# The norm of x and the input product of its convolution as filler of the first recurrence

## The chip, the cores and the metric

One core of one Trainium2 chip runs the whole program. The metric is device time of one execution in microseconds (us), less is better. The engines named below are PE (TensorE: matmuls and, beside them, weight loads, PEld), DVE (VectorE), ACT (ScalarE), POOL (GpSimd) and SP (SyncE, which issues nearly all DMAs).

## What is computed

Two blocks in a row on a sequence of 256 tokens of width 1024. The change lies in the first layer of the first block. Each layer of that block has a context `ctx` and a sequence `x`. Both are normalised, modulated by adaLN vectors, and multiplied by `w_in`; the first 1024 columns of the product go to a gated convolution, the rest to a recurrence (RWKV) in two directions. The recurrence of `ctx` runs first, and its final states are the initial states of the recurrence of `x`.

```python
mod_x = (silu_c @ ada_w[l] + ada_b[l])[:, None, :]        # six vectors: sh1 sc1 gt1 sh2 sc2 gt2
mod_c = silu_cc @ ada_w[l] + ada_b[l]
ux = modulate(rmsnorm(x, norm1_g[l]), sh1, sc1) @ w_in[l]
uc = modulate(rmsnorm(ctx, norm1_g[l]), csh1, csc1) @ w_in[l]
prep_c = rwkv_prep(uc[..., CONV_IN:], *rw)
yc, s_f, s_b = rwkv_scans(prep_c, s_zero, s_zero, emit=not last)
prep_x = rwkv_prep(ux[..., CONV_IN:], *rw)
yx, _, _ = rwkv_scans(prep_x, s_f, s_b, emit=True)
mix_x = concatenate([conformer_conv(ux[..., :CONV_IN], *cv), rwkv_out(yx, prep_x, *post)])
x = x + gt1 * (mix_x @ w_out[l])
x = x + gt2 * swiglu(modulate(rmsnorm(x, norm2_g[l]), sh2, sc2), ffn_wg[l], ffn_wu[l], ffn_wd[l])
# and the same for ctx
```

## The kernel before

Activations lie feature-major: a tile is 128 features by 256 tokens, and a float32 matrix is carried as a high and a low part, so that a product of one 128 x 128 weight tile is three matmuls (`mm3`). Every weight block of 512 KB is loaded by a DMA on SP into one of four `raw` buffers and then split by ACT (line 341, `wh`) and DVE (line 342, `wl`). Only the adaLN weights go from `raw` to PE unsplit.

The kernel is written as one program in Python; a planner orders each engine's instructions when the program is built. It goes by program order as the priority and by the times at which its own model expects operands and buffers. On the chip every engine then follows that fixed order. So an instruction that stands late in the program can be put early where nothing ahead of it is expected to be ready, if its buffer is free. Tiles of one tag share a fixed number of buffers: `S` has 20 (`NS`, line 46), the PSUM tag `pb` two, `T1b` six, `Sb` two, `z` two, the convolution's `tap` two.

The first layer's recurrence over `ctx` is `wide(0, cf, None, QB, False, norm_x)` (line 1461). `rwkv` (mode "wide") makes the input product, per-pair operands `AR` and `BK`, a triangular inverse on DVE (`inverse`, a loop of 31 steps of two small operations at lines 961 and 963, then small matmuls into `Q`), the tiles `GR`, `KB` (`reads`) and `uv`, `r0` (`values`), and then four steps of `chain` for each of two groups. After each of these eight steps, `fill(FILL)` (line 919, `FILL` = 6) takes six steps from a generator of other work, the filler. In the program before, the filler is `conv_in` of `ctx` (line 659; four steps, each a product with two weight blocks, a sigmoid on ACT, a multiply on DVE) and then `ada_steps` (line 478; sixteen steps, for the adaLN vectors 2 to 5: eight halves of four weight blocks each, every half a PSUM tile, a copy to `T2b` on ACT at line 497, eight tiny matmuls into a second PSUM tile and an add on DVE at line 503). All PSUM tiles of the filler are of tag `pb`.

At "post" (line 924), once the chain's steps are in the program, `norm_x` loads x into two `z` tiles, normalises it (`rms_blocks`, line 409), transposes it on PE (line 438, four `pb` tiles of four transposes) and writes it as four `S` tiles (`feature_major`, line 428, by the list `EVAC1`: a scaling into `T1b` on ACT or DVE, a high part on ACT at line 460, a low part on DVE or POOL at line 462). Behind it stand the recurrence's own group norm and gate (which load `gup`, line 927, into another `S` tile), the convolution of `ctx` (`conv`, line 700: taps on POOL, DVE and ACT), `mixed_in`, then `conv_in` of x into `zx` (lines 1468 to 1470; its adaLN list is empty), `w_in` of x, `out` for `ctx` (`wout`, line 1475), and the recurrence of x.

The `S` tiles are asked for in this order: input product (3), `dup`, `iup`, two `sg`, four `BK`, `Lo`, four `AR`, `tj`, `X`, then four pairs of `GR` and `KB`, `qt`, `qc`, two `Q` (line 984), `yall` (line 902), the four of x's norm, and `gup`.

Of the kernel before, what the change touches and what calls it, by code (L numbers as in the profile page):

```python
# [37 lines left out]
NPOOL, NPOOLE, NPOOLC = (14, 3), (12, 4), (30, 0)  # L38
NTAP = 2

QB, QE, QC, EVERY = (2, 3, 4, 5), (2, 3, 4, 5), (1,), 2

FILL = 6
LATER = 1500
# [214 lines left out]
class Prog:  # L259
# [1151 lines left out]
    def first(self):  # L1411
        nc = self.nc
        self.setup()
        RW = list(range(NRW))
        KWV = [4, 5, 6, 7, 8, 9, 10, 11, 12]
        drain = lambda g: [None for _ in g]
        alone = {"r": ("ps", "acc00", "acc01"), "t": ("acc10", "acc11"), "b": ("pb",), "c": ("acc11",), "cs": ("acc10",)}
        beside = {"r": ("ps",), "t": ("ps",), "b": ("pb",), "c": ("pb",), "cs": ("pb",)}
        self.pstags = {"r": ("ps", "pb", "acc00", "acc01", "acc10", "acc11"), "b": ("pb",)}

        fl = lambda t: t.rearrange("p (a b) -> p a b", a=4)
        z = lambda: self.t(self.pool, [P, 4, T], "z", bufs=2)

        def wide(l, x, s0, ada, perm, before=None):

            def filler():

                steps = itertools.chain(self.conv_in(l, x, fl(self.x[0])), self.ada_steps(l, ada))

                def fill(n=1):  # L1430
                    lane = self.lane
                    self.on("b")
                    for _ in range(n):
                        next(steps, None)
                    self.on(lane)

                return fill

            self.pstags = alone
            for at in self.rwkv(l, self.w_in(l, x, RW), s0, True, "wide", filler()):  # L1440
                if at == "post" and before is not None:
                    before()
            self.on("c")
            drain(self.conv(l, fl(self.x[0]), fl(self.x[1]), (NPOOL, NPOOLE)[l]))
            self.pstags = beside
            self.on("b")
            return self.mixed_in(fl(self.x[1]), self.y, perm)

        self.ada(0, (1, 0))
        cf = self.load("ctx")  # L1450
        nc.sync.dma_start(self.const[:, NCONST1:], self.ap["const"][:, NCONST1:])
        cf = self.norm1(0, cf, 1, False, self.xf)
        early = []

        def norm_x():
            zt = lambda: self.t(self.pool, [P, D], "z", bufs=2)
            self.on("b")
            early.append(self.norm1(0, self.load("x", [zt(), zt()]), 0, False, self.Sr, keep=True))
            self.on("r")

        cm = wide(0, cf, None, QB, False, norm_x)
        states = self.states
        self.on("b")
        (xf,) = early
        zx = z()
        mods = self.ada_steps(0, [q for q in (2, 3, 4, 5) if q not in QB])
        for _ in self.conv_in(0, xf, zx):
            next(mods, None)
            next(mods, None)
        drain(mods)  # L1470
        win = self.w_in(0, xf, RW)
        ux = next(win)
        drain(win)
        self.load("ctx", self.x)
        f = self.out(0, self.x, 1, cm)
        self.on("r")
        drain(self.rwkv(0, iter((ux, 0)), states, True, "half"))
        y = self.y
        self.on("b")
        acc = z()  # L1480
        self.go = False
        self.bg = self.conv(0, zx, acc, NPOOLC, True)
        self.mods, self.every = self.ada_steps(1, QC), EVERY
        self.ffn_add(0, self.x, 1, f)
        drain(self.mods)
        self.gn()
        self.ada(1, [q for q in (1, 0) if q not in QC])
        self.on("b")
        cf = self.norm1(1, self.x, 1, False, self.Sr, acc=True)
        self.on("r")  # L1490
        drain(self.rwkv(1, self.w_in(1, cf, KWV, "b"), None, False, "all"))
        states = self.states
        self.on("b")
        xm = self.mixed_in(acc, y)
        self.load("x", self.x)
        f = self.out(0, self.x, 0, xm)
        self.ffn_add(0, self.x, 0, f)
        self.on("r")
        for b in range(2):
            nc.sync.dma_start(self.keep[b], self.x[b])  # L1500
        xf = self.norm1(1, self.x, 0, True, self.xf, acc=True)
        xm = wide(1, xf, states, QE, True)
        for b in range(2):
            nc.sync.dma_start(self.x[b], self.keep[b])
        f = self.out(1, self.x, 0, xm)
        self.ffn_add(1, self.x, 0, f)
        self.rms_blocks(self.x, keep=True)
# [130 lines left out]
```

## Time and profile before

| | us |
|---|---|
| median of 3 runs | 2772.72 |
| lowest and highest of the runs | 2772.6 and 2775.5 |
| the profiled execution | 2776.2 |
| its span, first to last instruction | 2774.1 |
| mean granted TensorE clock of the profiled execution | 0.961 |

The span is what the rows below measure from; 2.1 us of the profiled execution lie outside it. A clock of 1.00 is 2.4 GHz and 0.50 is 1.2 GHz, the two levels that PE is granted. The first recurrence with everything around it lies between 110 and 440 us of the span.

### The profile page before, as it was taken

To read this page: it belongs to the slowest core of one execution; us is meant where nothing else is said; L and a number is where in the kernel's file an instruction comes from. 1 tells how busy PE (TensorE), PEld (TensorE's weight loads), DVE (VectorE), ACT (ScalarE), POOL (GpSimd) and SP (SyncE) were. 2 spreads that over 40 slices of the span, in tenths; PEclk is the share of its full clock that TensorE was granted. 3 is DMA by queue.
4 is the path that set the end of the run, shared out by engine and by line. 5 is a ranking of instruction groups with operands and counts; after the bars stand their busy time and mean duration, and the time that the engine had idled before them with its cause. 6 is when DMAs were issued, how large, how long until landed. Compare 5 with 4: busy or idle time off the path is not lost.

```text
span 2774.1 us, 53770 instructions
## 1 busy us (share of the span) xinstructions
PE 2628.3 (95%) x22398; PEld 2288.3 (82%) x22398; DVE 1713.4 (62%) x2703; ACT 1327.6 (48%) x2015; POOL 667.0 (24%) x669
## 2 busy tenths in 40 slices
PE   7889988999889998899899899999999999999998
PEld 4866867888678897866799899889899898889897
DVE  3885778655577555984555655666655655755655
ACT  5533654434564346433544544654544544644543
POOL 0287999920130001384200000010000000100000
PEclk9989989999999999979899999999999999999999
DMA  7244424434323354234355555524555554525653
GB/s 251 102 153 167 153 86 167 139 129 145 137 77 115 130 181 148 100 138 153 124 188 183 198 184 188 188 86 157 183 186 186 183 186 172 170 85 183 205 185 119
DMA packets 118767, 430.70 MB, mean 155 GB/s; under 512 B 13174, under 2 KB 13686, under 8 KB 118524
## 3 DMA queue, kind: packets, MB, share of 16 engines
q1 hardware_dynamic: 118524, 427.28, 44.7%
q8 instruction: 175, 2.87, 0.4%
q14 instruction: 68, 0.56, 0.1%
HBM read 425.13 MB, written 2.10 MB: 154 GB/s over the span
## 4 chain that ended last, share of the span: by engine, by line
PE 76%; DVE 10%; POOL 5%; ACT 5%; issue 2%; DMA 2%; SPq 0%; ACTq 0%; POOLq 0%; DVEq 0%
PE pb L333 32%; PE acc L333 24%; PE ps L333 19%; POOL tap L731 3%; DVE wl L342 2%; POOL z L732 1%; DVE T1c L725 1%; DMA raw<-in_ada 1%; DVE S L963 1%; DVE T L961 1%; POOL x L732 1%; ACT wh L341 1%; PE acc L438 0%; DMA raw<-in_wr 0%; ACT L384 0%
## 5 line engine op out<-in xcount | busy, mean ns | idle before, releaser
L342 DVE TENSOR_TENSOR wl<-raw,wh 128x1024 fp32r<-128x1024 f32 (+1 forms) x654 | 814.5, 1249 | 621.6 <-ACT wh L341 390.9
L341 ACT CAST wh<-raw 128x1024 fp32r<-128x1024 f32 (+1 forms) x654 | 681.8, 1046 | 892.7 <-PE pb L333 349.8
L333 PE MATMUL pb<-xf,wh 128*128 128x256 f32 (+1 forms) x2560 | 488.1, 289 | 15.6 <-DVE T1b L588 5.2
L333 PE MATMUL pb<-S,wh 128*128 128x256 f32 x2560 | 490.9, 289 | 4.3 <-DVE S L462 1.8
L333 PEld LDWEIGHTS pb<-xf,wh 128*128 128x128 f32 (+1 forms) x2560 | 411.3, 195 | 29.7 <-DVE T1b L588 8.8
L333 PEld LDWEIGHTS pb<-S,wh 128*128 128x128 f32 x2560 | 407.7, 192 | 21.5 <-issue 11.7
L333 PE MATMUL ps<-S,wh 128*128 128x256 f32 x2048 | 390.6, 288 | 0.5 <-ACT S L460 0.4
L333 PE MATMUL pb<-xf,wl 128*128 128x256 f32 (+1 forms) x1280 | 372.8, 292 | 8.9 <-DVE wl L342 8.9
L365 POOL TENSOR_TENSOR wl<-raw,wh 128x1024 fp32r<-128x1024 f32 x22 | 52.1, 2379 | 1340.7 <-ACT wh L364 824.2
L333 PE MATMUL pb<-S,wl 128*128 128x256 f32 x1280 | 367.4, 287 | 2.1 <-DVE wl L342 2.1
L333 PEld LDWEIGHTS ps<-S,wh 128*128 128x128 f32 x2048 | 327.0, 192 | 9.4 <-issue 3.7
L333 PE MATMUL ps<-S,wl 128*128 128x256 f32 x1024 | 293.8, 287 | 0.6 <-DVE wl L342 0.6
L333 PEld LDWEIGHTS pb<-xf,wl 128*128 128x128 f32 (+1 forms) x1280 | 249.3, 195 | 16.9 <-DVE wl L342 11.7
L333 PEld LDWEIGHTS pb<-S,wl 128*128 128x128 f32 x1280 | 245.3, 192 | 7.0 <-issue 3.2
L333 PE MATMUL acc<-wh,T 128*128 128x512 f32 x704 | 206.3, 393 | 0.0
L333 PEld LDWEIGHTS ps<-S,wl 128*128 128x128 f32 x1024 | 196.7, 192 | 3.0 <-issue 1.5
L333 PE MATMUL acc<-wh,T1b 128*128 128x512 f32 x528 | 158.6, 399 | 3.5 <-ACT T1b L341 3.5
L731 POOL TENSOR_SCALAR tap<-z,cols 128x255 f32<-128x255 f32 (+14 forms) x120 | 154.4, 1295 | 0.0
L333 PEld LDWEIGHTS acc<-wh,T 128*128 128x128 f32 x704 | 127.0, 189 | 23.6
L731 POOL TENSOR_SCALAR tap<-x,cols 128x246 f32<-128x246 f32 (+6 forms) x104 | 112.9, 1093 | 46.1 <-DVE x L670 46.0
L333 PEld LDWEIGHTS acc<-wh,T1b 128*128 128x128 f32 x528 | 94.9, 190 | 22.3 <-ACT T1b L341 4.4
L333 PE MATMUL acc<-wl,T 128*128 128x512 f32 x352 | 113.3, 395 | 0.0
(445 smaller groups left out, 3956.7 us busy)
## 6 DMA issues: line engine op xcount, KB each, us to landing
raw<-in_fu SPq DMA_DIRECT2D x132, 512.0 KB, 3.2
raw<-in_ada SPq DMA_DIRECT2D x96, 512.0 KB, 4.2
raw<-in_pu SPq DMA_DIRECT2D x88, 512.0 KB, 4.3
raw<-in_qu SPq DMA_DIRECT2D x88, 512.0 KB, 4.2
raw<-in_fd SPq DMA_DIRECT2D x66, 512.0 KB, 3.2
raw<-in_wr SPq DMA_DIRECT2D x51, 512.0 KB, 3.9
raw<-in_pd SPq DMA_DIRECT2D x44, 512.0 KB, 4.3
raw<-in_qd SPq DMA_DIRECT2D x44, 512.0 KB, 4.3
```

Of the source, the lines that this page charges most:

```text
L333: return self.nc.tensor.matmul(out, lhsT, rhs, start=start, stop=stop, **kw)
L341: self.nc.scalar.copy(hi, src)
L342: self.nc.vector.tensor_sub(lo, src, hi.bitcast(F32))
L365: self.nc.gpsimd.tensor_sub(lo, r, hi.bitcast(F32))
L725: nc.vector.scalar_tensor_tensor(av[:, d], z[:, f, s], w(j), av[:, d], ALU.mult, ALU.add)
L731: nc.gpsimd.tensor_scalar(t[:, d], z[:, f, s], w(j), None, ALU.mult)
L732: nc.gpsimd.tensor_add(zc[f][:, d], zc[f][:, d], t[:, d])
L961: nc.vector.tensor_mul(tv, tj[:, k + 1 : 32, k : k + 1].broadcast_to([P, m, k + 1]), X[:, k : k + 1, 0 : k + 1].broadcast_to([P, m, k + 1]))
L963: nc.vector.tensor_sub(X[:, k + 1 : 32, 0 : k + 1], X[:, k + 1 : 32, 0 : k + 1], tv)
```

## The change

The filler's second part becomes a generator that is passed to `wide`. For the first layer it is `then_x`: x's load and norm are one step; then `zx` is taken and the sixteen steps of adaLN run with the four steps of x's `conv_in` among them, one after the second of every four. The call at "post" and the loop behind `wide` that made x's `conv_in` go away. The second layer's `wide` gets the same sixteen adaLN steps as before. The first layer's filler has 4 + 1 + 16 + 4 = 25 steps of the 48 that are asked for, where it had 20.

```diff
-QB, QE, QC, EVERY = (2, 3, 4, 5), (2, 3, 4, 5), (1,), 2
+QC, EVERY = (1,), 2
...
-        def wide(l, x, s0, ada, perm, before=None):
+        def wide(l, x, s0, steps, perm):
...
-                steps = itertools.chain(self.conv_in(l, x, fl(self.x[0])), self.ada_steps(l, ada))
+                all_ = itertools.chain(self.conv_in(l, x, fl(self.x[0])), steps)
...
-            for at in self.rwkv(l, self.w_in(l, x, RW), s0, True, "wide", filler()):
-                if at == "post" and before is not None:
-                    before()
+            drain(self.rwkv(l, self.w_in(l, x, RW), s0, True, "wide", filler()))
...
-        def norm_x():
+        def then_x():
+
             zt = lambda: self.t(self.pool, [P, D], "z", bufs=2)
-            self.on("b")
             early.append(self.norm1(0, self.load("x", [zt(), zt()]), 0, False, self.Sr, keep=True))
-            self.on("r")
-
-        cm = wide(0, cf, None, QB, False, norm_x)
+            yield
+            early.append(z())
+            mods, conv = self.ada_steps(0, (2, 3, 4, 5)), self.conv_in(0, *early)
+            for i, _ in enumerate(mods):
+                yield
+                if i % 4 == 1:
+                    next(conv, None)
+                    yield
+            yield from conv
+
+        steps = then_x()
+        cm = wide(0, cf, None, steps, False)
+        drain(steps)
         states = self.states
         self.on("b")
-        (xf,) = early
-        zx = z()
-        mods = self.ada_steps(0, [q for q in (2, 3, 4, 5) if q not in QB])
-        for _ in self.conv_in(0, xf, zx):
-            next(mods, None)
-            next(mods, None)
-        drain(mods)
+        xf, zx = early
         win = self.w_in(0, xf, RW)
...
-        xm = wide(1, xf, states, QE, True)
+        xm = wide(1, xf, states, self.ada_steps(1, (2, 3, 4, 5)), True)
```

## Rows read from the trace of the kernel before

**Rows 1.** The page: the span, and busy time of each engine

```profile
span 2774.1 us, 53770 instructions
PE 2628.3 (95%) x22398; PEld 2288.3 (82%) x22398; DVE 1713.4 (62%) x2703; ACT 1327.6 (48%) x2015; POOL 667.0 (24%) x669
```

**Rows 2.** Windows by stage: stretch and length, then the columns of the heading

```profile
core 0: us, PE busy (x) PEld busy (x) DVE busy (x) ACT busy (x) POOL busy (x), PEclk, DMA share, GB/s
112.00:165.00 53.00, 42.45 (x496) 37.53 (x494) 48.60 (x101) 22.63 (x40) 31.10 (x31) 0.93 0.34 114
165.00:188.00 23.00, 22.70 (x186) 12.17 (x188) 21.03 (x56) 5.91 (x11) 14.70 (x15) 0.80 0.65 225
188.00:210.00 22.00, 22.00 (x382) 17.23 (x379) 10.85 (x16) 10.29 (x15) 19.16 (x23) 0.66 0.27 98
210.00:270.00 60.00, 58.41 (x803) 39.84 (x802) 35.26 (x73) 20.75 (x42) 47.19 (x54) 0.92 0.50 175
270.00:312.00 42.00, 42.00 (x261) 33.09 (x260) 26.78 (x44) 27.40 (x40) 38.28 (x40) 1.00 0.30 103
312.00:354.00 42.00, 41.55 (x312) 38.41 (x310) 31.44 (x46) 23.54 (x37) 41.38 (x42) 1.00 0.57 192
386.00:412.00 26.00, 14.97 (x205) 12.69 (x205) 24.02 (x38) 16.26 (x36) 25.92 (x20) 0.78 0.13 43
```

**Rows 3.** Timeline of POOL: the two clears of the `Q` tiles, line 986

```profile
188.18 0.95 POOL L986 MEMSET S<- 128x1024 f32 x1 [1.27 <-PE acc L333]
...
190.53 0.95 POOL L986 MEMSET S<- 128x1024 f32 x1 [0.72 <-DVE S L968]
```

**Rows 4.** Timeline of SP: loads of x, of its convolution's weights, of `gup`

```profile
107.06 0.33 SPq L1523 DMA_DIRECT2D z<-in_x  x1
...
242.83 10.43 SPq L348 DMA_DIRECT2D raw<-in_wc  x6
253.31 0.43 SPq L927 DMA_DIRECT2D S<-in_gup  x1
```

**Rows 5.** Windows of the adaLN matmuls alone: PE busy, loads, ACT, POOL, clock

```profile
166.70:211.00 44.30, 13.58 (x48) 1.58 (x48) 0.00 (x0) 0.00 (x0) 0.73 0.44 152
211.00:252.00 41.00, 16.59 (x64) 2.43 (x64) 0.00 (x0) 0.00 (x0) 0.90 0.60 211
```

**Rows 6.** The same for tile `T2b` (adaLN's tiny matmuls): PE, loads, ACT

```profile
166.70:211.00 44.30, 2.88 (x19) 2.62 (x20) 1.76 (x3) 0.73 0.44 152
```

**Rows 7.** Timeline of PE: adaLN matmuls of four weight blocks, and of one

```profile
159.04 1.92 PE L333 MATMUL pb<-raw,csil 128*32 128x512 f32 x16
...
177.27 1.05 PE L333 MATMUL pb<-raw,csil 128*32 128x512 f32 x4
```

**Rows 8.** Groups by line on PE, 252 to 312: transposes of x

```profile
L438 PE MATMUL pb<-const,z 128*128 128x128 f32 x12 | 1.7, 282 | 0.0
```

**Rows 9.** Windows between changes of the clock; columns as in rows 2

```profile
171.70:185.40 13.70, 13.45 (x142) 7.83 (x144) 11.80 (x32) 4.24 (x8) 8.46 (x9) 1.00 0.82 277
188.80:195.60 6.80, 6.80 (x163) 5.36 (x164) 6.47 (x8) 6.18 (x8) 6.08 (x7) 1.00 0.55 213
195.60:219.50 23.90, 23.90 (x258) 16.37 (x258) 12.67 (x26) 5.58 (x11) 20.36 (x26) 0.50 0.07 24
```

**Rows 10.** Timeline of PE: last matmuls of a `w_in` word, first of `wout`

```profile
351.04 0.40 PE L333 MATMUL pb<-S,wh 128*128 128x256 f32 x2
351.28 0.28 PE L333 MATMUL pb<-S,wl 128*128 128x256 f32 x1
351.40 0.86 PE L333 MATMUL acc<-wh,xf 128*128 128x512 f32 x3
```

**Rows 11.** Timeline of DVE: the last operation of `mixed_in` for ctx

```profile
316.47 0.47 DVE L342 TENSOR_TENSOR xf<-x,xf 128x256 fp32r<-128x256 f32 x1
```

**Rows 12.** Waits of PE, 112 to 165, and of all engines, 385 to 440

```profile
PE pb L333 <- DVE wl L342: 3.6, 3, 1.9
...
PE ps L333 <- DVE S L849: 3.4, 2, 2.8
```

More of the change, by code (lines that the diff above doesn't have):

```diff
@@ L1433, in fill @@
                     for _ in range(n):
-                        next(steps, None)
+                        next(all_, None)
                     self.on(lane)
```

## The prediction

> **What bounds the kernel now.** I read the page first, then windows by stage over the stretch that the change touches, then the timelines of single lines in it. PE is busy for 95% of the span [rows 1], so a change pays here only where it takes idle time or slow time from PE. The stage windows say where there is any [rows 2]. From 112 to 165 DVE is the bound (48.60 of 53 us, the inverse and the convolution's taps) and PE idles 10.55 us. From 165 to 188 DVE is still full (21.03 of 23) and PE is covered. From 188 to 354 PE is busy nearly throughout: 22.00 of 22, 58.41 of 60, 42.00 of 42, 41.55 of 42. Then, from 386 to 412, it idles 11 us behind the residual of `ctx` and its norm. So x's `conv_in`, which the change moves, stands in a stretch where PE has no gaps, and goes into one (210 to 270) where PE has 1.6 us of gaps. PE's work from 165 to 354 is a queue that is never empty: what counts is whether the new order makes PE idle, or lets it do the same work faster.
>
> **Part 1: x's load and statistics.** x is loaded at 107.06 [rows 4], although `norm_x` stands behind the chain in the program: the planner already put it where DMA and ACT had room. Nothing to gain there, 0 us.
>
> **Part 2: x's transposes and their evacuation.** Before, these came behind adaLN, because adaLN was ahead of them for the two `pb` buffers. Now they come ahead of it. The transposes themselves: 12 cost 1.7 us [rows 8], so 16 cost 2.3 us, and they can go into PE's idle time before 165 [rows 2]: **-2.3 us**. The evacuation is the point of this case. It writes four `S` tiles, and `S` is full. The clears of the two `Q` tiles show it: a clear needs no operand, only a buffer, yet POOL sat idle before the first until a matmul on PE, and before the second until the transpose of `X` on DVE [rows 3]: both waited for another `S` tile to be let go. In the order of the requests `yall` and then x's four tiles come next, so none of them can be had before 190.53. By the program the next ones let go are `qt` behind the inverse's first small matmuls, `BK` of pair 2, then `Lo` and `qc` behind its last ones (about 209), then `BK` of pair 3. `gup`, next in the order behind x's four, agrees: its load has no operand to wait for and is ahead in the program of x's `conv_in`, yet six blocks of that were issued before it, and it went at 253.31 [rows 4], when the first group's chain let its `AR` go. So x's high and low parts cannot be complete before about 210 to 216. Until then six `T1b` hold scaled tiles, the last transposed tile cannot be scaled and keeps one of the two `pb` buffers, and the other goes to the first half of adaLN, and then to x's first product, which waits for x.
>
> **Part 3: adaLN.** What follows is that between 166.7 and 211 only the first half of adaLN is left as filler, whose matmuls came at 159.04 before [rows 7]. Before, this stretch held 13.58 us of adaLN matmuls (12 blocks) [rows 5] and 2.88 us of tiny ones [rows 6], 16.5 us in all, and these now come behind 211. Not all of it is lost. From 188 to 210 PE was full and the inverse's small matmuls shared it with one block's 1.05 us and a pair's 1.9 us [rows 7], so the chain can start about 3 us sooner; and the last of `values`, about 3 us, can fill the room. I take 16.5 - 3 - 3 = **+10.5 us**. The ends: 0, if x's tiles get buffers sooner than I read, and 16.5.
>
> On the other side, blocks that wait for PE are cheaper than blocks that PE waits for. Two blocks of one half use different columns of the array: the 16 matmuls of four blocks took 1.92 us where they came together, 0.12 us each, and the 4 of one block 1.05 us where it came alone, 0.26 each [rows 7]. In 166.7 to 252 the 112 took 30.17 us [rows 5], nearly all alone; together they would take 13.4, so the gain lies between 0 and 16.8 us. Behind the change blocks pile up while the banks are held, but after the first few the fixed order again takes them as the planner expects them. I take a quarter: **-4 us**.
>
> The Trainium skill's page Perfetto Trace Analysis, section Optimization Strategy, speaks for and against the change at once: it advises interleaving stretches with different bounds, and says that bubbles which repeat can mean that there is no memory for the next tile. Rows 3 agree with the second; by the first alone part 3 would cost nothing.
>
> **Part 4: x's input product.** Eight blocks of 24 matmuls at 0.12 us, the pace of the last word of `w_in` [rows 10]: 23.0 us. They leave 259 to 309 and enter 211 to about 295, and PE is full in both: 0. Now their splits stand in the queues of ACT and DVE between the chain's own operations, and a product that waits for a low part holds the chain's matmuls behind it. The nearest row is the same work on `ctx`: 3.6 us of PE's waits for `wl` while DVE was full [rows 12]. DVE is at 35.26 of 60 in the chain [rows 2], so I take **+1.5 us** between 0 and 3.6. The eight DMAs change places with adaLN's on SP; at 0.50 DMA share [rows 2] that costs nothing.
>
> **Part 5: who waits for a later chain.** With 23 us of product and the adaLN of part 3 ahead of the chain's last two steps in priority, the chain ends up to 23.0 + 10.5 - 4 - 2.3 = 27 us later than before. Behind it come the group norm and `mixed_in`, whose last operation began at 316.47 [rows 11], and `wout`, which did not wait for it: PE reached it at 351.40, straight from `w_in` [rows 10]. The cover is 34.5 us, so this costs 0, and 1 us for each us by which the chain's delay exceeds 34.5. `gup` comes later with the chain, but is first needed after it.
>
> **Part 6: POOL.** The taps for x begin when those for `ctx` let go of the two `tap` buffers, with or without `zx`; an earlier `zx` can save at most POOL's 3.7 idle us of 270 to 312 [rows 2]. POOL's delay shows on PE once, in the 3.4 us wait for line 849 [rows 12]. I take **-1 us** between -3.4 and 0. Fewer switches between sigmoid and silu on ACT are covered by PE: 0.
>
> **The sum.** -2.3 + 10.5 - 4 + 1.5 - 1 = +4.7 us. The profiled execution's span goes from 2774.1 to 2778.8 us and its time from 2776.2 to 2780.9. The median lies 3.5 us under that execution, so I forecast 2777.4 us, slightly slower, and just under 0.2% (5.5 us), about what a measurement of this kernel can tell from no change. With the parts' own ends the forecast's case spans 2768 to 2787.
>
> **The rivals.**
>
> *Slower: the inverse is left bare.* Between 171.7 and 195.6 PE ran at 2.4 GHz but for one short stretch, and from 195.6 to 219.5 at 1.2 GHz [rows 9], where adaLN had thinned out and the inverse's small matmuls ran. If, without adaLN, the clock is down from about 172 on, the two full-speed stretches, 20.5 us, do half the work. About 10 us of it was adaLN's, which is gone; so the rest just fits, nothing is pulled forward, and the inverse's matmuls of 188.8 to 195.6 take some 4 us more. Then +16.5 + 4 - 2.3 + 1.5 - 1 = +18.7, without the gain from pairs: 2791 us. It decides from the point where less than 11 us of the 16.5 come back. For it speaks that PE has little else there; against it, that the clock came back to full twice in it [rows 9].
>
> *Faster: blocks in pairs.* If blocks arrive in pairs for most of the remaining 28, three quarters of 16.8 are -12.6 in place of -4: -3.9. If the product also lifts the clock as soon as it starts, some 8 us of the 23.9 at 1.2 GHz [rows 9] become 4: -8. So about 2765 us. Against it: the fixed order was built for blocks that come one by one.
>
> *Faster: the product holds the clock.* If the buffers come earlier than I read, x's product runs inside 195.6 to 219.5, the 23.9 us at 1.2 GHz become 12, part 3 costs nothing, and the sum is -12 - 2.3 + 1.5 - 1 = -13.8: 2759 us. The skill's page TensorE: Matmul & The Clock Gate, section HAM oscillation, says so as a rule: idle gaps of PE drop the clock, steady work keeps it. The trace agrees only in part: PE is shown busy for 23.90 of these 23.9 us [rows 9].
>
> *No effect.* The planner had hoisted x's load already and could keep the rest nearly as it was, with x's tiles behind adaLN for want of buffers: 2773 us.
>
> **How the numbers follow.** Forecast 0.47, bare inverse 0.24, pairs 0.12, clock held 0.10, no effect 0.07. The forecast's case lies within 0.2% with 0.33 of its 0.47, above with 0.12, below with 0.02. Faster by over 0.2%: 0.12 + 0.10 + 0.02 = 0.24; within: 0.33 + 0.07 = 0.40; slower: 0.12 + 0.24 = 0.36. The range is 2759 to 2793: it reaches the slower rival and the faster ones, and leaves out the chance that parts of two rivals add up.
>
> **What would show it.** Right: x's transposes near 160; its high parts (line 460) no earlier than 200; hardly any adaLN on PE between 170 and 210 and idle time or a low clock there; the chain's end near 290; `wout` starting straight after `w_in`, near 356. Part 2 is wrong if line 460 runs before 195. Part 5 is wrong if PE idles before `wout` for `mixed_in`. The sum is wrong, with its steps right, if PE takes the remaining blocks in pairs, or if the windows of 165 to 220 show another clock than I took.

## The result and the profile after

The changed kernel is slower: a median of 2808.78 us (2804.9 to 2812.5) against 2772.7 us of the kernel before on the same chip, a ratio of 1.0124 (95% interval 1.0104 to 1.0143). The forecast was 2777.4 us and its range ended at 2793. The profiled execution of the changed kernel, at the upper end of its runs, has a span of 2810.5 us, 36.4 more than [rows 1].

Here is what came of the rows ahead of the prediction. First the span and the engines, from the page of the changed kernel:

```profile
span 2810.5 us, 53763 instructions
PE 2650.6 (94%) x22398; PEld 2314.4 (82%) x22398; DVE 1712.9 (61%) x2703; ACT 1319.9 (47%) x2010; POOL 657.6 (23%) x669
```

The instructions of PE are as many as before, and they are busy 22.3 us longer; the other 14 us are idle time. The stage windows of the changed kernel (stretch and length, then busy time and count of PE, weight loads, DVE, ACT and POOL, granted clock, DMA share, GB/s) answer to [rows 2]:

```profile
112.00:165.00 53.00, 41.91 (x483) 38.22 (x482) 48.77 (x102) 22.97 (x41) 31.37 (x31) 0.90 0.26 92
165.00:188.00 23.00, 19.18 (x186) 15.35 (x185) 22.97 (x56) 9.03 (x16) 18.07 (x17) 0.65 0.37 137
188.00:210.00 22.00, 19.35 (x298) 16.80 (x298) 15.72 (x26) 8.73 (x13) 21.20 (x25) 0.50 0.01 3
210.00:270.00 60.00, 58.39 (x784) 43.49 (x784) 26.27 (x53) 17.83 (x37) 54.10 (x65) 0.90 0.46 161
270.00:312.00 42.00, 42.00 (x319) 28.76 (x315) 19.06 (x35) 14.58 (x23) 30.80 (x33) 0.96 0.67 237
312.00:354.00 42.00, 39.11 (x273) 34.72 (x273) 32.30 (x51) 24.13 (x39) 41.14 (x43) 0.96 0.41 141
```

From 165 to 210 PE idles 6.5 us where it idled 0.3, and the DMA share of 188 to 210 fell from 0.27 to 0.01: no weights are fetched, as the `raw` buffers hold blocks that wait. Windows of the adaLN matmuls alone (PE busy, its loads, ACT, POOL, clock) against [rows 5], and the two sides of the place where the clock came back, against [rows 9]:

```profile
166.70:211.00 44.30, 1.92 (x16) 0.42 (x16) 0.00 (x0) 0.00 (x0) 0.58 0.20 73
211.00:252.00 41.00, 7.17 (x32) 1.12 (x32) 0.00 (x0) 0.00 (x0) 0.86 0.36 129
252.00:305.00 53.00, 15.43 (x80) 2.43 (x80) 0.00 (x0) 0.00 (x0) 0.97 0.65 226
```

```profile
174.60:222.40 47.80, 40.10 (x580) 34.81 (x576) 36.82 (x70) 17.10 (x31) 44.51 (x47) 0.50 0.11 42
222.40:270.10 47.70, 47.70 (x597) 33.49 (x596) 18.64 (x39) 13.45 (x27) 43.76 (x52) 1.00 0.58 203
```

Four blocks of adaLN ran under the inverse where 16 had run (those of 159.04 and the twelve behind [rows 5, 7]). On the other side all 128 matmuls now take 1.92 + 7.17 + 15.43 = 24.5 us, against 1.92 + 13.58 + 16.59 = 32.1 before: they come in fours of blocks more often. The longest half-speed stretch doubled, from 23.9 to 47.8 us. Line 460, x's high parts, in the changed kernel (count, durations in ns, first and last start):

```profile
L460 ACT CAST S<-T1b x8: 401/404/408, 221.3 to 224.5; 128x256 fp32r<-128x256 f32 x8
```

And the timeline of the changed kernel at x's first squaring on ACT, at the weight loads and `gup` in SP's queue, and at the last matmul of `w_in` and the first of `wout`, against [rows 4, 10]:

```profile
111.84 0.64 ACT L416 ACTIVATE sq<-z 128x512 f32<-128x512 f32 x1 [1.14 <-DMA z<-in_x]
...
169.99 0.80 SPq L348 DMA_DIRECT2D raw<-in_wc  x2
170.88 63.55 SPq L348 DMA_DIRECT2D raw<-in_ada  x8
...
264.34 0.42 SPq L927 DMA_DIRECT2D S<-in_gup  x1
...
365.81 0.28 PE L333 MATMUL pb<-S,wl 128*128 128x256 f32 x1
365.93 0.86 PE L333 MATMUL acc<-wh,xf 128*128 128x512 f32 x3
```

The issues of eight loads of adaLN stretch over 63.55 us of the queue, from 170.88 on. `wout` starts at 365.93 in place of 351.40. So **14.5 us** arise up to `wout`. The other 22 us arise behind it, where the program's text did not change:

| us of the profiled execution | before | after | |
|---|---|---|---|
| D: x's first squaring to `wout` of ctx | 239.6 | 254.1 | +14.5 |
| A: from there to x's squaring in the second layer (1066.2; 1085.5) | 714.8 | 719.6 | +4.8 |
| B: from there to x's `wout` in that layer (1320.3; 1353.6) | 254.1 | 268.1 | +14.0 |
| C: from there to the end | 1453.8 | 1456.9 | +3.1 |

### The profile page after: what moved, and what is told of

It is laid out like the page before. It is cut to its first block, busy times and chain, and to the rows that moved or that the text cites. A ratio compares the mean times of both kernels' runs of the same rounds, so it can differ in the third digit from the quotient of the medians.

```text
span 2810.5 us, 53763 instructions
## 1 busy us (share of the span) xinstructions
PE 2650.6 (94%) x22398; PEld 2314.4 (82%) x22398; DVE 1712.9 (61%) x2703; ACT 1319.9 (47%) x2010; POOL 657.6 (23%) x669
## 4 chain that ended last, share of the span: by engine, by line
PE 78%; DVE 12%; ACT 4%; POOL 2%; issue 2%; DMA 2%; ACTq 0%; DVEq 0%; POOLq 0%
PE pb L333 33%; PE acc L333 25%; PE ps L333 20%; DVE wl L342 2%; DVE T1c L725 2%; DVE S L963 1%; DVE T L961 1%; POOL tap L731 1%; ACT wh L341 1%; POOL x L732 1%; PE acc L438 0%; DMA raw<-in_ada 0%; ACT L384 0%; DVE acc L619 0%; DMA raw<-in_wr 0%
## 5 line engine op out<-in xcount | busy, mean ns | idle before, releaser
L333 PE MATMUL pb<-xf,wh 128*128 128x256 f32 (+1 forms) x2560 | 485.1, 287 | 12.4 <-ACT T1b L585 4.2
L333 PEld LDWEIGHTS pb<-S,wh 128*128 128x128 f32 x2560 | 411.0, 194 | 25.8 <-issue 14.2
L731 POOL TENSOR_SCALAR tap<-z,cols 128x255 f32<-128x255 f32 (+14 forms) x120 | 147.0, 1233 | 0.0
```

Source lines behind the costliest of these rows:

```text
L333: return self.nc.tensor.matmul(out, lhsT, rhs, start=start, stop=stop, **kw)
L731: nc.gpsimd.tensor_scalar(t[:, d], z[:, f, s], w(j), None, ALU.mult)
```

## The experiments

All kernels are measured in these four stretches (the time ahead of D differs by a few us from run to run). The ratio is to the kernel before on the same chip, with its 95% interval.

| run | D | A | B | C | ratio |
|---|---|---|---|---|---|
| before | 239.6 | 714.8 | 254.1 | 1453.8 | |
| swap_vectors | 241.0 | 709.6 | 257.5 | 1453.7 | 1.0001 (0.9991 to 1.0010) |
| after | 254.1 | 719.6 | 268.1 | 1456.9 | 1.0124 (1.0104 to 1.0143) |
| after_swap | 255.1 | 716.5 | 260.6 | 1454.5 | 1.0102 (1.0084 to 1.0119) |
| after_fill8 | 255.1 | 716.5 | 262.1 | 1452.8 | 1.0091 (1.0076 to 1.0106) |
| after_fill5 | 254.0 | 717.8 | 260.7 | 1457.6 | 1.0090 (1.0075 to 1.0105) |
| norm_only | 241.2 | 719.6 | 259.6 | 1451.9 | 1.0028 (1.0014 to 1.0042) |
| norm_then_ada | 242.2 | 715.8 | 257.9 | 1453.9 | 1.0048 (1.0032 to 1.0065) |
| turns_late | 248.0 | 713.4 | 253.7 | 1454.2 | 1.0001 (0.9989 to 1.0013) |
| ada8_first | 248.2 | 710.1 | 269.0 | 1453.2 | 1.0062 (1.0043 to 1.0081) |
| own_after | 254.3 | 712.9 | 262.2 | 1458.9 | 1.0078 (1.0060 to 1.0097) |
| own_before | 250.0 | 717.8 | 259.1 | 1452.7 | 1.0054 (1.0033 to 1.0075) |
| product_no_dve | 243.1 | 710.4 | 264.9 | 1453.9 | 1.0014 (1.0000 to 1.0027) |
| conv_late | 224.1 | 736.4 | 260.7 | 1454.4 | 1.0011 (0.9995 to 1.0027) |
| fill5 | 238.3 | 715.0 | 265.1 | 1453.7 | 1.0045 (1.0030 to 1.0059) |
| fill8 | 242.9 | 721.9 | 270.2 | 1448.9 | 1.0082 (1.0067 to 1.0097) |

D is steady where the first part's order is kept: the changed kernel and its three variants lie between 254.0 and 255.1. Edits that move nothing of the change (swap_vectors, fill5, fill8) put it between 238.3 and 242.9, so a difference of 3 us in D says little. Three questions were put.

**Which of the three moves costs the 14.5 us?** First the norm alone, on the kernel before:

```diff
-steps = itertools.chain(self.conv_in(l, x, fl(self.x[0])), self.ada_steps(l, ada))
+steps = itertools.chain(self.conv_in(l, x, fl(self.x[0])), before, self.ada_steps(l, ada))
...
-cm = wide(0, cf, None, QB, False, norm_x)
+cm = wide(0, cf, None, QB, False, norm_x())
```

> The kernel before, with the norm of x as the filler's first step of the second part and nothing else moved: adaLN follows in a row, x's input product stays behind the recurrence. Theory (first place holds the banks, and the product in turn takes the second one): one bank is held by x's last transposed tile, but adaLN has the other to itself, so blocks go on one after the other; half of the cost up to wout, 5 to 9 us, wout at 356 to 361 us. Rival (the norm alone does it): wout at 364 to 368 us with a half-speed stretch of 45 us or more. Rival (the turns alone do it): wout at 349 to 354 us.

D came to 241.2, +1.6: the norm in front is nearly free, and the rival that lays it on the turns is right (`wout` at 349.8). Windows of this run, first of the clock, then of adaLN alone:

```profile
168.00:188.50 20.50, 19.65 (x135) 10.57 (x133) 14.59 (x41) 2.63 (x5) 13.33 (x14) 0.50 0.51 183
...
195.30:219.20 23.90, 23.43 (x339) 19.10 (x333) 15.40 (x29) 8.76 (x15) 20.42 (x24) 0.50 0.01 2
```

```profile
166.70:211.00 44.30, 10.41 (x32) 1.11 (x32) 0.00 (x0) 0.00 (x0) 0.59 0.38 137
```

From 160 to 225 us the mean clock is 0.65 in this run, 0.74 before and 0.58 in the changed kernel. So more than half of what the changed kernel lost in clock is here too, and yet D lost 1.6 us: adaLN went on, at the slow clock. The clock alone is not the price. Then the changed kernel without the turns:

```diff
-            for i, _ in enumerate(mods):
-                yield
-                if i % 4 == 1:
-                    next(conv, None)
-                    yield
+            yield from mods
             yield from conv
```

> The changed kernel without the turns: the filler takes the norm of x, then all sixteen adaLN steps in a row, then the four of x's input product. Theory (the product in turn waits for S): the product asks for a bank only when x is long there, adaLN goes through by the other bank as in the run with the norm alone, distance 239 to 245 us. Rival (the product in the chain): it is enough that the product stands ahead of the chain's last steps: 250 us or more.

D is 242.2, as the theory had it. The copies that end adaLN's halves (line 497) show the difference; up to 200 us the run without turns has three, the changed kernel one:

```profile
L497 ACT COPY T2b<-pb x3: 586/586/587, 171.4 to 189.4; 128x512 f32<-128x512 f32 x3
```

```profile
L497 ACT COPY T2b<-pb x1: 585/585/585, 170.9 to 170.9; 128x512 f32<-128x512 f32 x1
```

Then the turns, put off until behind five halves (turns_late), and the norm put off until behind four (ada8_first):

```diff
-                if i % 4 == 1:
+                if i > 8 and i % 2 == 1:
```

> The changed kernel with the turns put off: the filler takes the norm of x, then five halves of adaLN (ten steps), and only then x's input product in turns, one step behind each further half. Theory (PE's order under the inverse): the first product stands in PE's fixed order ahead of adaLN's second half and waits for operands from DVE, which the inverse keeps full until 188 us; put behind five halves it waits for nothing. Distance from x's first squaring to wout's first matmul 240 to 246 us (before 239.6, after 254.1, adaLN in a row 242.2), and three halves of adaLN copied out before 200 us. Rival (the turns themselves cost, by the banks or by the product ahead of the chain): 250 us or more.

```diff
+            mods = self.ada_steps(0, (2, 3, 4, 5))
+            for _ in range(8):
+                next(mods)
+                yield
             zt = lambda: self.t(self.pool, [P, D], "z", bufs=2)
...
```

> The changed kernel, but the filler takes eight adaLN steps (four halves) first, then the norm of x, then the other eight in turns with x's input product. Theory (first place holds the banks): the cost up to wout comes only from x's transposed tiles holding a pb bank while the S tiles are full, so that adaLN is missing under the inverse. With four halves ahead they run at 160 to 200 us as before, the half-speed stretch of PE between 160 and 225 is about 24 us long and not 48, line 460 comes at 200 to 225, and wout's first matmul at 349 to 354 us (before 351.4, after 365.9). Rival (turns): the alternation of adaLN blocks with the product is what costs, wherever the norm stands: wout at 360 or later. For the rest of the program, from wout's first matmul to the end (before 2422.7, after 2444.6 us): theory (order) says it moves by 5 us or more in either direction although its work is the same, rival (lateness) says it goes back to 2423 within 4 us, together a time of 2773 within 5 us.

248.0 and 248.2: between theory and rival in both, so both were incomplete. In turns_late the three halves came before 200 us as expected (the third at 195.9), and D still lost 5.8 us to the run without turns. Windows of the whole of D, in the kernel before, in the changed kernel, in turns_late and in norm_then_ada (columns as in the stage windows):

```profile
111.81:351.40 239.59, 226.70 (x2411) 176.64 (x2411) 171.91 (x328) 108.68 (x181) 189.21 (x201) 0.91 0.44 152
```

```profile
111.84:365.93 254.09, 232.02 (x2411) 187.79 (x2410) 171.55 (x328) 103.91 (x178) 208.38 (x222) 0.87 0.40 143
```

```profile
112.97:361.01 248.04, 231.74 (x2415) 187.28 (x2414) 170.53 (x328) 102.81 (x177) 196.72 (x211) 0.87 0.43 146
```

```profile
111.44:353.63 242.19, 225.95 (x2418) 180.58 (x2417) 168.51 (x328) 101.27 (x176) 198.50 (x211) 0.92 0.44 151
```

PE idles 12.9, 22.1, 16.3 and 16.2 us in them. Of the 14.5 us, 9.2 are idle time of PE, and for 5.3 its matmuls are busy longer, at a mean clock of 0.87 in place of 0.91. The step from turns_late to the changed kernel, 6.0 us, is idle time of PE (5.8 us): the price of a product ahead of adaLN's second half under the inverse. The step from norm_then_ada to turns_late, 5.8 us, is none: PE idles alike and is busy 5.8 us longer, at a mean clock of 0.87 in place of 0.92. So it is not made of waits for products among the steps of the chain, and products run there in norm_then_ada too (256.6 to 284.4, the chain's last state at 292.3). Why PE had the lower clock in this one execution stays open. What is left, 1.6 to 2.6 us for the norm, is no more than D moves by without it. The fourth half of ada8_first came out at 198.8 and the fifth at 236.1 (the norm now stands in the way behind 200 us), so its +8.6 is no clean repeat of either step.

**What does the product wait for?** The prediction said: for x's `S` tiles. A first pair gives x's norm a place of its own, in both kernels (and the scratch tile `sq` becomes bfloat16):

```diff
+            one = new([P, T], F32R)
+            hs = ls = [one.unsqueeze(1).broadcast_to([P, 4, T])] * 2
...
-early.append(self.norm1(0, self.load("x", [zt(), zt()]), 0, False, self.Sr, keep=True))
+early.append(self.norm1(0, self.load("x", [zt(), zt()]), 0, False, self.own, keep=True))
```

> The changed kernel, with x's norm written to memory of its own and not to S tiles. There is room for 1 KB per partition only, so all eight high and low parts go to one place over each other: the instructions and their sizes stay, the numbers that x's products read don't. Measured as the distance from x's first squaring to wout's first matmul (before 239.6, after 254.1, adaLN first 248.2, norm alone 241.2 us). Theory (the product in turn waits for S): with tiles of its own line 460 is done by about 175, x's product and adaLN both run under the inverse, the half-speed stretches between 160 and 225 add up to less than 30 us (after: 54.6), and the distance is 236 to 243 us. Rival (the turns themselves): the product's matmuls ahead of the chain cost, whatever it waits for: 250 us or more.

> The kernel before with the same memory of its own for x's norm, beside the run of the changed kernel with it. In the kernel before adaLN stands ahead of x's norm, so that nothing in the first recurrence waits for x's S tiles: distance from x's first squaring to wout's first matmul 237 to 242 us by both theories. The rest of the program, of which S tiles are freed earlier, is open by both, some 2420 to 2445 us.

The tiles did come earlier, and D did not move: 254.3. The mean clock of 160 to 225 us was 0.63 (0.58 in the changed kernel), which makes 48 of these 65 us at half speed where under 30 were expected. Here are the high parts in own_after (line 464 there) and the low parts on DVE (466), and then the timeline of PE at the product:

```profile
L464 ACT CAST xn<-T1b x8: 398/405/420, 158.8 to 184.5; 128x256 fp32r<-128x256 f32 x8
L466 DVE TENSOR_TENSOR xn<-T1b,xn x6: 407/410/473, 164.3 to 186.2; 128x256 fp32r<-128x256 f32 x6
```

```profile
186.74 0.79 PE L333 MATMUL pb<-xn,wh 128*128 128x256 f32 x2
...
192.06 0.40 PE L333 MATMUL pb<-xn,wh 128*128 128x256 f32 x2
194.24 0.73 PE L333 MATMUL ps<-S,S 32*32 32x32 f32 x18 [1.79 <-DVE S L973]
...
219.84 0.58 PE L333 MATMUL pb<-xn,wl 128*128 128x256 f32 x1
...
226.72 1.07 PE L333 MATMUL pb<-raw,csil 128*32 128x512 f32 x8
```

The last high part came at 184.5 and not at 224.5, so the full `S` was indeed what had held line 460. But behind it stood the next wait: four scalings and six low parts had to find room on DVE, which the inverse keeps full. The product began at 186.74, its second half at 219.84 behind the inverse's and `values`' matmuls in PE's fixed order, and adaLN's second half behind it at 226.72. The pair is not clean, as own_before missed its expectation by 8 us (250.0): with high and low parts in one place each must wait for the one before, 10.6 us in a row there. So a second run takes DVE out of x's product altogether:

```diff
+            if new == self.own and op == "l":
+                continue
+            e = "A" if new == self.own else e
...
+        if whole:
+            st = (self.raw(f"wc{l}", i) for i in range(8))
...
+                        self.mm(pu[:, j, :], w[:, k * P : k * P + P], x[k][0].bitcast(F32), k == 0, k == NF - 1)
```

> The changed kernel with an input product of x that needs nothing of DVE: x's tiles in the 1 KB of their own, scaled and written by ACT alone, without the low parts, and the product as one plain float32 matmul by the unsplit block in place of three by its parts (adaLN's blocks are multiplied so). The low parts of x are left out and its tiles lie over each other. Theory (the product waits for DVE): its first step runs before 182 us, adaLN's second half follows before 195, the half-speed stretches between 160 and 225 add up to 35 us or less (after 54.6), and the distance is 238 to 248 us, though the plain product itself is longer. Rival (the turns themselves): 252 us or more.

D is 243.1, with the same turns in the same places. PE in this run, at x's first product and the adaLN behind it, then the clock:

```profile
172.58 4.00 PE L333 MATMUL pb<-xn,raw 128*128 128x256 f32 x10
...
176.83 2.43 PE L333 MATMUL pb<-xn,raw 128*128 128x256 f32 x10
...
180.08 2.86 PE L333 MATMUL pb<-xn,raw 128*128 128x256 f32 x12
182.87 1.06 PE L333 MATMUL pb<-raw,csil 128*32 128x512 f32 x8
```

```profile
176.70:186.90 10.20, 9.85 (x118) 7.32 (x117) 10.16 (x21) 2.50 (x5) 6.72 (x7) 1.00 0.37 122
186.90:221.10 34.20, 33.91 (x458) 27.16 (x462) 20.02 (x40) 12.53 (x20) 30.13 (x36) 0.50 0.20 73
```

The product ran under the inverse and adaLN followed, though only half of the half (the rest at 209.99, not before 195), and the half-speed stretches were 41 us and not 35. Its window of D:

```profile
110.62:353.67 243.05, 231.95 (x2354) 182.13 (x2353) 155.68 (x310) 94.90 (x172) 193.96 (x215) 0.89 0.44 151
```

D fell by 11.0 us against the changed kernel, and PE's idle time in it from 22.1 to 11.1. So some 11 of the 14.5 us go with what the product needs of its operands, x's tiles and the split weights. The run doesn't only take a wait away: DVE does 18 operations less (155.7 us in place of 171.6) and ACT 9.0 us less, so wait and work are not told apart. The 3.5 us that stay with the turns are of the size by which D moves without them. The waits were under the inverse and not in the chain: from 220 to 366 us PE in the changed kernel waited once, and that for the shift behind `w_in`:

```profile
PE pb L333 <- DVE S L630: 2.9, 1, 2.9
```

How much is DVE's and how much is that of `S` in the changed kernel itself is not separated further: own_after took only `S` away, product_no_dve both.

**Where do the 22 us behind `wout` come from?** Two edits that change no work, only how many filler steps stand behind a step of the chain (in both layers' `wide`), on the kernel before:

```diff
-FILL = 6
+FILL = 5
```

> The kernel before with five filler steps behind a step of the chain in place of six: the same work, nearly the same order in the first recurrence, but the planner orders the rest of the program anew. Theory (order): wout's first matmul within 5 us of 351.4, and the rest from there on differs from 2422.7 us by 5 us or more, in either direction, with no cause in the edit. Rival (lateness): the rest is within 4 us of 2422.7 and the time within 5 us of 2773.

> The kernel before with eight filler steps behind a step of the chain in place of six: again the same work and a new order later on. Theory (order): wout's first matmul within 6 us of 351.4, and the rest differs from 2422.7 us by 5 us or more. Rival (lateness): the rest is within 4 us of 2422.7 and the time within 6 us of 2773.

A + B + C, 2422.7 before, became 2433.8 and 2441.0, and the ratios are 1.0045 and 1.0082: a re-ordering that does little to the first recurrence (D 238.3 and 242.9) costs up to 0.8%. In fill5 `wout` came at 345.2, 1.2 us further off than expected, as all ahead of D was 4.9 us shorter. The counterpart is an edit that leaves the order of the rest alone:

```diff
-QB, QE, QC, EVERY = (2, 3, 4, 5), (2, 3, 4, 5), (1,), 2
+QB, QE, QC, EVERY = (2, 3, 5, 4), (2, 3, 4, 5), (1,), 2
```

> The kernel before with two adaLN vectors of the first recurrence's filler in the other order (2, 3, 5, 4 for 2, 3, 4, 5): the same work, and an order of the engines that is the same but for those blocks, 120 lines of PE's, against 2600 to 5400 in the runs so far. Theory (order): the rest of the program keeps the order of the kernel before, so it keeps its time: distance to wout within 3 us of 239.6, rest from wout on within 3 us of 2422.7. Rival (any edit in this stretch, or the chip, costs the rest): 2428 us or more, as in the eight other runs (2427.6 to 2444.6).

2420.8, and a ratio of 1.0001. The same edits on the changed kernel:

> The changed kernel with eight filler steps behind a step of the chain in place of six: the same work, hardly another order in the first recurrence, the rest ordered anew. Theory (order): distance from x's first squaring to wout's first matmul within 4 us of 254.1, and the rest from wout on differs from the 2444.6 us of the changed kernel by 4 us or more, while it stays above the 2422.7 us of the kernel before as in the four runs so far (2431.1 to 2441.0). Rival (lateness): the rest stays within 3 us of 2444.6.

> The changed kernel with two adaLN vectors of the filler in the other order (2, 3, 5, 4 for 2, 3, 4, 5): the same work, and an order that differs from that of the changed kernel by 243 lines of PE's, all in the first part of the program. Theory (order): what the changed kernel lost behind wout belongs to the order that the planner made of the rest, so it stays here: distance from x's first squaring to wout within 3 us of 254.1, rest from wout on within 4 us of 2444.6, and a time of 2803 to 2813. Rival (the chip, or a single execution): the rest falls back by 8 us or more towards the mean of the other runs, 2431.

> The changed kernel with five filler steps behind a step of the chain in place of six: the same work, 2270 lines of PE's order other than in the changed kernel. Theory (order): distance from x's first squaring to wout within 5 us of 254.1, rest from wout on anywhere between 2421 and 2445 us, as in the runs so far, and 4 us or more from 2444.6. Rival (the rest is the late chain's own price): rest within 4 us of 2444.6.

The two FILL runs gave 2431.4 and 2436.1, away from 2444.6 as the order theory wants. But after_swap, which keeps the order of the changed kernel, gave 2431.7 and not 2444.6: its number falls to the rival, a single execution, and with it the two FILL runs are no evidence for the order. Most of what it lacks lies in stretch B. The window of B, in the changed kernel and in after_swap:

```profile
1085.50:1353.60 268.10, 237.25 (x2797) 182.51 (x2795) 187.40 (x360) 112.56 (x200) 126.57 (x144) 0.86 0.35 123
```

```profile
1082.60:1343.20 260.60, 227.53 (x2798) 175.52 (x2796) 186.39 (x359) 112.65 (x200) 126.82 (x144) 0.90 0.37 127
```

The same matmuls in the same order were busy 9.7 us less at a clock of 0.90 in place of 0.86. So some 7.5 us of B's +14.0 were the clock of that one execution. What is left is 6.5 to 8.0 us in the three variants. In after_swap and after_fill8 most of it is idle time of PE (33.1 and 32.8 us of B, 26.7 before), in after_fill5 only 2.3 us are (29.0); in the changed kernel PE idles 30.8.

Taken together: the two runs with the order of the kernel before have A + B + C at 2422.7 and 2420.8. Twelve programs with another order (conv_late, which moves work across the border, left aside) lie between 2421.3 (turns_late) and 2441.0, in the mean at 2431.6, and the profiled execution of the changed kernel above them. There is no tie to D: fill5 has the shortest D of them and loses 11 us, turns_late has +8.4 in D and loses none.

Three things limit what this shows. `FILL` also sets the filler of the second layer's recurrence, which is B, so the +11.0 and +16.1 us of fill5 and fill8 in B may be the edit's own doing there. Single executions of one order differ by several us: before and swap_vectors by 5.2 in A and 3.4 in B, the changed kernel and after_swap by 12.9 in A + B + C. And the four programs that have the instructions of the kernel before behind `wout`, only in another order (norm_only, norm_then_ada, turns_late, ada8_first), lie just -1.4 to +9.6 us from it. Their ratios go by all runs. Without their part in D these are between -0.3 and +0.4%, each more than the half width of its interval (0.2% at most). So a new order moves the rest either way, by up to 11 us in these four; which of the moved instructions does it in B wasn't settled.

Last, a try at using PE's idle time behind the residual of ctx:

```diff
         f = self.out(0, self.x, 1, cm)
+        zx = z()
+        drain(self.conv_in(0, xf, zx))
         self.on("r")
```

> The kernel before with x's input product behind the output product of ctx and no longer ahead of it, for the 11.7 us in which PE idles between the residual sum of ctx (385.6) and the first down product of its FFN (432.2). wout comes earlier by the product, a distance of 216 to 222 us, and the stage from the norm's first squaring to the first down product, 46.6 us before, grows by 11 to 15 us and not by 23, if the idle time takes the product: 8 to 12 us gained there. Theory (order): the rest is drawn anew and gives back 5 to 20 us, so 2766 to 2785 us in all. Rival (lateness): the gain stays, 2761 to 2766 us; it is lost if x's convolution, which starts 100 us later, isn't through when the FFN is.

D is 224.1: `wout` came 15.5 us earlier, less than the product's length and than expected, and the stage from the norm to the first down product grew from 46.6 to 71.1 us, by more than the product: PE idled 12.4 us there as before (11.7). The product found its place beside the idle time and not in it. The ratio is 1.0011, and the median of 2781.6 us lies where the order theory had it. No run beat the kernel before; turns_late, swap_vectors and conv_late are level with it.

## Why the prediction was wrong, point by point

**Part 1** (x's load and statistics, 0) was right: x's first squaring came at 111.84 against 111.81.

**Part 2** was right in its mechanism: the transposes came at 158.7 to 168.5, line 460 at 221.3 to 224.5 (forecast: 210 to 216, by no means before 200), `gup` at 264.34. Own_after confirms that `S` held it. The -2.3 us are there too, as the transposes are gone from behind the chain's start (2.4 us before). That norm_only gains nothing (+1.6) doesn't speak against it, since adaLN moved with the norm.

**Part 3** was right that only the first half of adaLN would run under the inverse, and here the sum up to `wout` failed: in what it counted as displaced and as coming back. It took 16.5 us, up to 211, for displaced, and 6 of these for coming back, by a chain 3 us sooner and by `values` in the room. The chain's first state came at 222.2 before and at 220.4 in the changed kernel. Windows up to it and behind it: all of PE, then the adaLN matmuls, then the tiny ones, each before and after (columns as in [rows 2, 5, 6]):

```profile
165.00:222.20 57.20, 56.90 (x670) 36.70 (x672) 42.79 (x92) 18.26 (x30) 44.10 (x49) 0.70 0.41 145
222.20:351.40 129.20, 127.16 (x1254) 102.22 (x1249) 80.33 (x137) 67.61 (x111) 114.00 (x122) 1.00 0.49 170
```

```profile
165.00:220.40 55.40, 47.33 (x634) 40.19 (x634) 45.39 (x93) 20.78 (x34) 48.19 (x52) 0.56 0.16 58
220.40:365.93 145.53, 142.62 (x1301) 109.23 (x1297) 77.23 (x135) 60.01 (x103) 128.82 (x141) 0.97 0.55 193
```

```profile
222.20:351.40 129.20, 11.40 (x52) 1.70 (x52) 0.00 (x0) 0.00 (x0) 1.00 0.49 170
```

```profile
220.40:365.93 145.53, 22.60 (x112) 3.55 (x112) 0.00 (x0) 0.00 (x0) 0.97 0.55 193
```

```profile
222.20:351.40 129.20, 4.22 (x32) 3.87 (x32) 2.34 (x4) 1.00 0.49 170
```

```profile
220.40:365.93 145.53, 7.27 (x56) 6.86 (x56) 4.10 (x7) 0.97 0.55 193
```

AdaLN stayed away until the chain began and not until 211. Behind that point it takes 14.2 us more (11.2 and 3.05), although its 128 matmuls gained 7.6 us by coming together, where -4 was taken. The chain began only 1.8 us sooner, and `values` did not fill the room: PE idled 8.1 us ahead of it, in place of 0.3. So the part came to 14.2 - 1.8 = +12.4 us in place of +10.5 - 4 = +6.5. What held adaLN's second half is not separated in the changed kernel. x's last transposed tile kept its `pb` bank until line 458 scaled it at 223.9 and the product had asked for the other, as Part 2 says; and in PE's order adaLN's second half (225.89) stands behind the product's first matmuls (222.91). In own_after the transposed tiles were out of their banks by 169.5, and adaLN's second half still came right behind the product, at 226.72: there PE's order was enough.

**Part 4** priced the waits of the product in the chain at +1.5 us, between 0 and 3.6. Behind the chain's start PE idles 2.9 us in the changed kernel and 2.0 before, +0.9, and its one wait there is for the shift behind `w_in`, not for the product: this part held.

**Part 5** was right: the chain's last state came at 286.1 for 269.2 (forecast near 290), and `wout` follows `w_in` directly; the cover held. **Part 6**: the first tap for x came 11 us earlier on POOL (265.4 for 276.5), and nothing on PE gained by it: the wait for line 849, 3.4 us before, is 6.9 us.

**The sum** up to `wout` was +4.7 and is +14.5: +12.4 for adaLN, -2.4 for the transposes, +0.9 for PE's idle time in the chain, and 3.6 us that the sum had no term for. They go with the clock: behind the chain's start its mean is 0.97 in place of 1.00, which makes about 9 of 145.5 us at half speed, worth at most 4.4 us by an estimate from these two numbers. The forecast's own span is not the sum of its parts' ends either: with the ends of the term for pairs these add up to -22.5 and +17.8, which is 2750 to 2790 and not 2768 to 2787.

**The larger miss is a step that wasn't written down**: that everything behind `wout` would keep its time. Its 22 us have no term in the sum, nor in the range, although the text says that a planner orders the whole program. A new order cost 9 us in the mean of the twelve programs (2431.6 - 2422.7). How the 22 divide between this order and single executions stays open: with the same order after_swap lies 27.4 us above the kernel before by the medians, the changed kernel 36.1.

**The rivals.** The bare inverse came nearest. It was forecast with a half-speed stretch from about 172 to 220, and there is one from 174.6 to 222.4; and little of the displaced work came back. Its +18.7 left out the gain from pairs, which is 7.6. The slow clock that it starts from is not the price by itself, as norm_only shows. The rival with the product that holds the clock isn't tested: in product_no_dve x's product ran under the inverse from 172.58 to 182.9, ahead of the stretch in question, with the clock at 1.00 from 176.7 to 186.9 and at half speed behind it, to 221.1.

The Trainium skill's page Perfetto Trace Analysis, section Optimization Strategy, says that interleaving stretches with different bounds may improve performance. It didn't here: D grew by 14.5 us in the changed kernel, and by 3.5 us in product_no_dve, where the product needs nothing of the engine that bounds the stretch.

## What to carry to other kernels

A filler is as good as its operands: what is to run under a stretch that DVE bounds should need nothing of DVE, nor of the buffers which that stretch holds, and on an engine with a fixed order a filler that isn't ready stands in the way of one that is. In a program that is ordered as a whole, put a term for the rest into the sum and its spread into the range: edit something that does no work and see what that costs (here -2, +11 and +18 us) before a difference of 10 us is laid to a change.

## What the runs showed of the hardware

PE can run at half speed although it is shown busy throughout. A window of ada8_first, from 190 to 222:

```profile
190.00:222.00 32.00, 32.00 (x470) 26.79 (x466) 18.38 (x34) 11.60 (x20) 26.37 (x31) 0.50 0.11 36
```

470 mostly small matmuls, 32.00 us busy of 32.00, and 1.2 GHz in all of it. In the kernel before the clock fell at 195.6 behind 6.80 us of which all were busy [rows 9]. The Trainium skill's page TensorE: Matmul & The Clock Gate, section HAM oscillation, ties the drop to idle gaps; in these stretches no gap is shown. And time at half speed is no price by itself: from 160 to 225 us the mean clock is 0.74 before and 0.65 in norm_only, and D differs by 1.6 us.
